# U weights' low parts by accumulating DMA during the gate build, and a scratch tensor for the first gate columns

## The chip, the cores and the metric

One core of a Trainium2 chip runs the kernel. The metric is the device time of one execution in microseconds (us). Before the change it is 1632.03 us, the median of three runs (1631.69 to 1634.06).

## The reference

One layer of a hybrid decoder trunk on 512 tokens of width 1024: state-space heads and attention heads side by side, an output projection and a normalisation, then a PEER mixer, and a last normalisation. The change lies in the mixer:

```python
q = (xb @ w_query).reshape(T, PEER_HEADS, 2, PEER_HALF_DIM)
s = jnp.einsum('thkd,hknd->thkn', q, sub_keys)
sv, si = lax.top_k(s, K)                       # K = 16, per half
...
top_s, top_pos = lax.top_k(cand_s, K)          # 16 of 256 candidate sums
expert_idx = jnp.take_along_axis(cand_i, top_pos, axis=-1)
gate = jax.nn.softmax(top_s, axis=-1)
u = jnp.take(u_table, expert_idx, axis=0)      # 16384 x 1024
act = jax.nn.gelu(jnp.einsum('td,thkd->thk', xb, u), approximate=False)
v = jnp.take(v_table, expert_idx, axis=0)
return jnp.einsum('thk,thkd->td', gate * act, v)
```

So each token has 128 experts (8 heads times 16), each with a gate.

## The kernel before

For the first 368 tokens (`NU`) the kernel doesn't gather experts. It computes the activations of all 16384 experts densely, in 128 *U chunks* of 128 experts, and multiplies them by a gate matrix that is zero except at the chosen experts; 128 *V chunks* then multiply the result by the V table. The last 16 tokens of the third block of 128 (`UG`) have their U part gathered row by row (`ug_index`, `ug_fetch`, `ug_dots`, `ug_head`), and the fourth block is gathered altogether during the V stage (`gather`).

**High and low parts.** Matmuls run on rounded 32-bit values (`F32R`). To keep accuracy, a weight tile `wir` of 128x1024 floats (512 KB) is split in two: ScalarE rounds it (`wih`, or `wihx` for each fourth tile), and another engine subtracts to get the remainder (`wil`). `mm3` then issues three matmuls, high times high, low activations times high weights, high activations times low weights; the low part is needed only in the third. The `Stream` class does the loads (on SP's DMA queue, three raw buffers), the roundings and the subtractions. When a chunk is about to be used, `get` has `splits` make the low part of the chunk two further on (`la = 2`, three `wil` buffers), and the rounding runs one more ahead (`ha = 1`). The subtraction is on GpSimd in the scoring stage and on VectorE from the index stage on (`lo_on`).

**A hand-written order.** The kernel is scheduled by hand: each engine runs its instructions in the order in which the program issues them. Two planner clocks, `tm[0]` for TensorE and `tm[1]` for VectorE, decide where U chunks go: `drive` issues a U chunk (`step_u`, 4.07 on TensorE's clock and, when VectorE subtracts, 1.2 on its own) whenever TensorE's clock isn't ahead, and otherwise the next piece of VectorE work. 54 U chunks (`LEAD`) come before the V stage, which then alternates U and V chunks.

**The stages around the change**, in order:

- *Index stage*, `stage2`: VectorE turns the chosen positions into expert indices, block by block (2, 0, 1, 3). After block 2 `ug_index` sends the indices of the 16 tokens to DRAM and back on GpSimd's queue (`ugi`, `ugg`, `uix`, `ugw`) and starts three row gathers (`urow`). After block 1 `g_head(0)` transposes indices and gates on TensorE and writes `ijT` and `gT`.
- *Gate build*, `build_g`: 48 steps of eight tokens. `hot` makes one-hot matrices on VectorE (`ij`, `g`; two buffers, one step ahead), 16 small matmuls form the gate columns, ScalarE copies them to `stg`, and after each fourth step SP stores 2 MB to the DRAM scratch `gsp`. The first 16 steps also each take the dot product of a gathered row (`urow`), and each frees its buffer for a further gather on GpSimd's queue.
- *Remaining U chunks* up to 54, then the V stage. `v_prep` multiplies activations by gate columns, which `load_g` reads back from `gsp` for four chunks at a time (`gt`), with the first two loads issued at the start of the V stage.

Of the kernel before, what the change touches and what calls it, by code (L numbers as in the profile page):

```python
# [11 lines left out]
F32 = mybir.dt.float32  # L12
# [5 lines left out]
AF = mybir.ActivationFunctionType  # L18
OP = mybir.AluOpType
AX = mybir.AxisListType  # L20
PSUM = bass.MemoryType.PSUM
# [9 lines left out]
NT = 384  # L31
UG = 16
NU = NT - UG
LEAD = 54
# [19 lines left out]
def tile_block(ctx: ExitStack, tc: tile.TileContext, I, out):  # L54
    nc = tc.nc
    ctx.enter_context(tc.manual_schedule())
    V, A, T, G = nc.vector, nc.scalar, nc.tensor, nc.gpsimd
# [3 lines left out]
    def pool(name, bufs=1, **kw):  # L61
        p = tc.alloc_tile_pool(name=name, bufs=bufs, **kw)
        opened.append(p)
        return p

    def close(*ps):
        for p in ps:
            opened.remove(p)
            p.release()

    def mm3(ps, lh, ll, rh, rl, start, stop):
        T.matmul(ps, lh, rh, start=start, stop=False)  # L72
        T.matmul(ps, lh, rl, start=False, stop=False)  # L73
        T.matmul(ps, ll, rh, start=False, stop=stop)  # L74

    def chain(*gs):
        for g in gs:
            yield from g

    class Stream:  # L80
        def __init__(self, p, name, srcs, shape, raw=2, la=1, lo=None, bufs=None):
            self.bufs = bufs or la + 1
            self.held, self.hold, self.place = (), None, {}
            self.lo = lo or (lambda n: V)
            self.p, self.name, self.srcs, self.shape, self.rawb, self.la = p, name, srcs, shape, raw, la
            self.raw, self.hi, self.w, self.nl, self.nh, self.ns, self.ha = {}, {}, {}, 0, 0, 0, 0
# [26 lines left out]
        def splits(self, m):  # L113
            while self.ns < min(m, len(self.srcs)):
                n = self.ns
                self.his(n + 1 + self.ha)
                r, h = self.raw.pop(n), self.hi.pop(n)
                l = self.tiles(n, 1)[:, :r.shape[-1]]
                self.lo(n).tensor_tensor(l, r, h, op=OP.subtract)  # L119
                self.w[n] = (h, l)  # L120
                self.ns += 1
                self.loads(n + 1 + self.rawb)
# [68 lines left out]

    dram = pool("dram", space=DRAM)
    xsp = dram.tile([NB, 128, D], F32, name="xsp")
    gsp = dram.tile([NT // 32, 128, 128, 32], F32, name="gsp")
    acd = dram.tile([64, 128], F32, name="acd")
    ugi = dram.tile([UG, 128], I32, name="ugi")
    ugg = dram.tile([UG, 128], F32, name="ugg")
# [26 lines left out]
    lo_on = [V]  # L224
# [14 lines left out]
    win = Stream(wst, "wi", items, [128, 1024], raw=3, la=2, lo=lambda n: lo_on[0])  # L239
    cnt = [0]  # L240

    def item():
        cnt[0] += 1
        return win.get(cnt[0] - 1)
# [17 lines left out]
    for p in range(2):  # L262
# [11 lines left out]
        for j, cs, act in (((0, slice(0, D), 1), (1, slice(0, D), 1)) if p == 0 else  # L274
                           ((0, slice(0, D), 0), (1, slice(0, 512), 1), (1, slice(512, D), 0))):
            t = XH[:, 2 * p + j, cs]
# [353 lines left out]
    for i in range(13, 18):  # L630
# [3 lines left out]
        q = qraw[i - 13] = wk.tile([128, S], F32, name="qr", bufs=5)  # L634
# [10 lines left out]
    for n in range(8):  # L645
# [3 lines left out]
        h, l = item()  # L649
# [89 lines left out]
    def qk_nope(h):  # L739
        wh, wl = item()  # L740
        ps = pp()
        for k in range(3):
            ks = slice(k * 128, k * 128 + 128)
            mm3(ps, wh[:, ks], wl[:, ks], qlh[:, k], qll[:, k], k == 0, k == 2)
        QN[h] = pair("qn")
        evac(ps, *QN[h])
        yield
        ps = pp()
        for k in range(2):
            ks = slice(384 + k * 128, 512 + k * 128)  # L750
            mm3(ps, wh[:, ks], wl[:, ks], kvh[:, k], kvl[:, k], k == 0, k == 1)
        KN[h] = pair("kn")
        evac(ps, *KN[h])
        yield
# [70 lines left out]
    g = chain(qk_nope(1), v_proj(0))  # L825
# [3 lines left out]
    for st in range(38):  # L829
        h, q = divmod(st, 4)  # L830
        if q == 0 and h:
            g = iter(())
            if h < 7:
                g = chain(qk_nope(h + 1), v_proj(h // 2)) if h % 2 == 0 else chain(q_pe(h // 2 + 1), qk_nope(h + 1))
# [34 lines left out]
    psX = pool("psX", bufs=2, space=PSUM)  # L869
    psW = pool("psW", bufs=4, space=PSUM)  # L870
# [227 lines left out]
    def build_g():  # L1098
        bc = [128, 4, 128, 2]

        def hot(n):
            ijT, gT = GT[n // 16]
            t0 = n % 16 * 8
            col = lambda z: z[:, t0:t0 + 8].rearrange("p (q c) -> p q c", c=2)[:, :, None, :].to_broadcast(bc)
            ij = gb.tile([128, 2, 4, 128, 2], F16, name="ij", bufs=2)
            g1 = gb.tile(bc, F16, name="g1", bufs=2)
            b2 = [128, 8, 128, 2]
            V.tensor_tensor(ij.rearrange("p e q i c -> p (e q) i c"), iotaE[:, None].to_broadcast(b2),  # L1108
                            ijT[:, n % 16].rearrange("p e (q c) -> p (e q) c", c=2)[:, :, None, :].to_broadcast(b2),
                            op=OP.is_equal)  # L1110
            oi, oj = ij[:, 0], ij[:, 1]
            V.tensor_tensor(g1, oi, col(gT[:, 1]), op=OP.mult)  # L1112
            V.tensor_tensor(oi, oi, col(gT[:, 0]), op=OP.mult)
            return oj, oi, g1

        nxt = hot(0)
        dots, head = ug_dots(), ug_head()
        tm[1] += 3.0
        yield 2.6
        for n in range(48):  # L1120
            b, g = divmod(n, 16)
            oj, oi, g1 = nxt
            if n < 47:
                nxt = hot(n + 1)
            if g % 4 == 0:
                stg = gb.tile([128, 128, 32], F32, name="stg", bufs=2)
            for hf in range(2):
                ps = pw()
                for t in range(4):
                    q, c = hf * 2 + t // 2, t % 2  # L1130
                    T.matmul(ps[:, t * 128:(t + 1) * 128], oj[:, q, :, c], oi[:, q, :, c], start=True, stop=False)
                    T.matmul(ps[:, t * 128:(t + 1) * 128], oj[:, q, :, c], g1[:, q, :, c], start=False, stop=True)
                q0 = g % 4 * 8 + hf * 4
                A.activation(stg[:, :, q0:q0 + 4],
                             ps.rearrange("p (t i) -> p i t", t=4), AF.Copy, scale=1.0 / GSC)
            tm[0] += 1.1
            if g % 4 == 3:
                for i in ((slice(0, 128),) if n < 47 else (slice(0, 8), slice(8, 128))):
                    nc.sync.dma_start(gsp[b * 4 + g // 4, :, i], stg[:, i])
            if g == 12 and b < 2:  # L1140
                g_head(b + 1)
            if n >= 1:
                tm[1] += next(dots, 0.0)
            if n in (30, 32, 34, 36, 38):
                tm[1] += next(head)
            yield 2.55 if n < 47 else 0.1
# [48 lines left out]
    def u_chunk(c, psum=None):  # L1195
        h, l = item()
        h = h.rearrange("p (k j) -> p k j", k=8)
        l = l.rearrange("p (k j) -> p k j", k=8)
        ps = (psum or pu)()[:, :NU]
        for k in range(8):  # L1200
            mm3(ps, h[:, k], l[:, k], XTH[:, k, :NU], XTL[:, k, :NU], k == 0, k == 7)
        ACT[c] = act_tile()
        A.activation(ACT[c][:, NU:], one, AF.Copy)
        A.activation(ACT[c][:, :NU], ps, AF.Gelu)  # L1204
# [5 lines left out]
    uc = 2  # L1210
# [26 lines left out]
    def step_u():  # L1237
        un[0] += 1
        u_chunk(un[0] - 1)
        tm[0] += T_U  # L1240
        if lo_on[0] is V:
            tm[1] += 1.2

    un = [uc]

    def drive(fill):
        while True:
            if tm[0] <= tm[1] and un[0] < (LEAD - RES if len(aps) > 1 else KEEP):
                step_u()
                continue  # L1250
            c = next(fill, None)
            if c is None:
                return
            tm[1] += c
# [24 lines left out]
    UR["g"] = ijp.tile([UG, 128], F32, name="ugw")  # L1279
    rt2 = pool("rt2")  # L1280
    lo_on[0] = V
    drive(stage2())
    close(rt2)
    close(rt)
    gb = pool("gb", side="right")
    UR["hd"] = gb.tile([128, UG], F32, name="uhd")
    UR["w"] = gb.tile([UG, 128], F32, name="uw")
    UR["m"] = gb.tile([UG, 2], F32, name="um")
    drive(build_g())
    uc = un[0]  # L1290
    while uc < LEAD:
        u_chunk(uc)
        uc += 1
    close(gb)
    close(psW)
    close(psX)

    psV = pool("psV", space=PSUM)
    va = [[psV.tile([128, 512], F32, name=f"va{b}{e}") for e in range(2)] for b in range(3)]
    vst = pool("vst")  # L1300
    gt = {}

    def load_g(q):
        if q < 32 and q not in gt:
            gt[q] = vst.tile([128, NT // 32, 4, 32], F32, name="gt", bufs=2)
            nc.sync.dma_start(gt[q], gsp[:, :, q * 4:(q + 1) * 4, :].rearrange("b j i t -> j b i t"))

    PP = {}

    pend = []  # L1310
# [23 lines left out]
    def v_lo():  # L1334
        if pend:
            c, P, Ph = pend.pop()
            Pl = v_sb(c, "Pl")
            V.tensor_tensor(Pl, P, Ph, op=OP.subtract)
            PP[c] = (Ph, Pl)

    def v_mm(b, c, hl, es=(0, 1)):
        Ph, Pl = PP[c]
        h, l = hl
# [250 lines left out]
```

## Time and profile before

| what | value |
|---|---|
| median of three runs | 1632.03 us |
| the profiled execution | 1631.69 us, span 1629.9 us |
| TensorE (PE) busy | 1582.4 us, 97% |
| VectorE (DVE) busy | 1376.6 us, 84% |
| ScalarE (ACT) busy | 699.2 us, 43% |
| GpSimd (POOL) busy | 467.8 us, 29% |
| DMA | 393.77 MB, mean 242 GB/s |

Busy time is what the profiler records for an engine; matmuls are pipelined, so that their recorded times overlap. "L119" is line 119 of the kernel. A row such as `wil<-wir,wih` names the output and the inputs by the program's tile names, followed by the shape and, in grouped views, the count, the total and the mean. In a timeline the first number is the start in us and the second the duration; a bracket at the end tells how long the engine stood idle before it and what ended the wait. POOL and SP rows named DMA are the issue of a transfer, not the transfer.

### The profile page before, as it was taken

To read this page: it belongs to the slowest core of one execution; us is meant where nothing else is said; L and a number is where in the kernel's file an instruction comes from. 1 tells how busy PE (TensorE), PEld (TensorE's weight loads), DVE (VectorE), ACT (ScalarE), POOL (GpSimd) and SP (SyncE) were. 2 spreads that over 40 slices of the span, in tenths; PEclk is the share of its full clock that TensorE was granted. 3 is DMA by queue.
4 is the path that set the end of the run, shared out by engine and by line. 5 is a ranking of instruction groups with operands and counts; after the bars stand their busy time and mean duration, and the time that the engine had idled before them with its cause. 6 is when DMAs were issued, how large, how long until landed. Compare 5 with 4: busy or idle time off the path is not lost.

```text
span 1629.9 us, 23745 instructions
## 1 busy us (share of the span) xinstructions
PE 1582.4 (97%) x8640; PEld 1394.0 (86%) x8640; DVE 1376.6 (84%) x2649; ACT 699.2 (43%) x1213; POOL 467.8 (29%) x332
## 2 busy tenths in 40 slices
PE   7999989999999999999899999999999999999997
PEld 5777868888888999998799999999999999888886
DVE  8979688947799999999588888888888888988977
ACT  5575466641433445555333333333333333333331
POOL 0000000000133113200155545555454544544300
PEclk9999999999999999999999999999999999999999
DMA  6242121364423368766799999999999999999973
GB/s 244 91 156 91 46 64 49 107 236 142 135 91 91 117 185 304 274 234 244 241 358 348 350 327 343 344 351 331 328 353 346 344 326 353 357 339 338 337 223 122
DMA packets 149020, 393.77 MB, mean 242 GB/s; under 512 B 12360, under 2 KB 63000, under 8 KB 147112
## 3 DMA queue, kind: packets, MB, share of 16 engines
q1 hardware_dynamic: 105816, 237.76, 43.1%
q0 software_dynamic: 42944, 154.24, 26.2%
q8 instruction: 67, 1.10, 0.3%
q14 instruction: 49, 0.40, 0.1%
q10 hardware_dynamic: 144, 0.26, 0.0%
HBM read 359.66 MB, written 31.51 MB: 240 GB/s over the span
## 4 chain that ended last, share of the span: by engine, by line
PE 72%; DVE 21%; ACT 2%; DMA 2%; issue 2%; SPq 0%; DVEq 0%; ACTq 0%
PE va L1347 10%; PE va L1351 10%; PE va L1348 10%; PE pu L72 8%; PE pu L74 8%; PE pu L73 8%; PE pa L72 3%; PE pa L74 3%; PE pa L73 3%; DVE wil L119 3%; DVE ij L1108 2%; DVE g L1112 1%; DVE t L952 1%; DVE urow L1053 1%; DVE ti L956 1%
## 5 line engine op out<-in xcount | busy, mean ns | idle before, releaser
L109 ACT ACTIVATE wih<-wir 128x1024 fp32r<-128x1024 f32 (+2 forms) x269 | 277.8, 1034 | 261.1 <-DMA wir<-v 87.4
L119 DVE TENSOR_TENSOR wil<-wir,wih 128x1024 fp32r<-128x1024 f32 (+1 forms) x254 | 302.1, 1190 | 103.4 <-ACT wih L109 47.2
L74 PE MATMUL pu<-XTH,wil 128*128 128x368 f32 x1008 | 331.7, 329 | 0.7 <-DVE wil L119 0.7
L72 PE MATMUL pu<-XTH,wih 128*128 128x368 f32 x904 | 298.8, 331 | 0.0
L73 PE MATMUL pu<-XTL,wih 128*128 128x368 f32 x904 | 296.8, 328 | 0.0
L1348 PE MATMUL va<-wil,Ph 128*128 128x512 f32 x726 | 283.5, 390 | 0.0
L1384 POOL DMA_INDIRECT row<-u,ix x128 | 189.9, 1484 | 231.2 <-DVE row L1395 135.7
L1384 POOL DMA_INDIRECT row<-v,ix x128 | 183.6, 1434 | 194.7 <-DVE ac L1401 165.5
L74 PEld LDWEIGHTS pu<-XTH,wil 128*128 128x128 f32 x1008 | 189.0, 188 | 1.3 <-DVE wil L119 1.3
L72 PEld LDWEIGHTS pu<-XTH,wih 128*128 128x128 f32 x904 | 169.7, 188 | 2.9
L73 PEld LDWEIGHTS pu<-XTL,wih 128*128 128x128 f32 x904 | 169.6, 188 | 2.9
L1347 PE MATMUL va<-wih,Ph 128*128 128x512 f32 x432 | 168.5, 390 | 0.0
L1401 DVE SCALAR_TENSOR_TENSOR ac<-row,hd,ac 128x1024 f32<-128x1024 f32 x128 | 164.1, 1282 | 2.5 <-DMA row<-v,ix 0.3
L1348 PEld LDWEIGHTS va<-wil,Ph 128*128 128x128 f32 x726 | 136.9, 189 | 26.1
L1204 ACT ACTIVATE act<-pu 128x368 f32<-128x368 f32 x126 | 60.0, 476 | 227.5 <-PE pu L74 193.3
L1395 DVE SCALAR_TENSOR_TENSOR row<-row,x 128x1024 f32<-128x1024 f32 x128 | 150.0, 1220 | 1.4 <-DMA row<-u,ix 1.4
L109 ACT ACTIVATE wihx<-wir 128x1024 fp32r<-128x1024 f32 x67 | 71.1, 1061 | 157.4 <-DMA wir<-v 124.6
L1351 PE MATMUL va<-wih,Pl 128*128 128x512 f32 x432 | 133.3, 390 | 0.0
L1347 PE MATMUL va<-wihx,Ph 128*128 128x512 f32 x294 | 115.9, 394 | 4.8 <-ACT Ph L1331 4.8
L119 DVE TENSOR_TENSOR wil<-wir,wihx 128x1024 fp32r<-128x1024 f32 x62 | 75.9, 1224 | 52.3 <-issue 47.8
L1351 PEld LDWEIGHTS va<-wih,Pl 128*128 128x128 f32 x432 | 81.1, 188 | 17.3
L1347 PEld LDWEIGHTS va<-wih,Ph 128*128 128x128 f32 x432 | 81.1, 188 | 15.7
(458 smaller groups left out, 3072.6 us busy)
## 6 DMA issues: line engine op xcount, KB each, us to landing
wir<-ut SPq DMA_DIRECT2D x128, 512.0 KB
wir<-v SPq DMA_DIRECT2D x128, 512.0 KB
gt<-gsp SPq DMA_DIRECT2D x32, 768.0 KB
gsp<-stg SPq DMA_DIRECT2D x11, 2048.0 KB
wir<-wo SPq DMA_DIRECT2D x26, 512.0 KB
wir<-wf SPq DMA_DIRECT2D x18, 512.0 KB
wir<-wqr SPq DMA_DIRECT2D x16, 512.0 KB
de<-acd POOLq DMA_DIRECT2D x8, 512.0 KB
```

What stands on the lines that cost most here:

```text
L72: T.matmul(ps, lh, rh, start=start, stop=False)
L73: T.matmul(ps, lh, rl, start=False, stop=False)
L74: T.matmul(ps, ll, rh, start=False, stop=stop)
L109: A.activation(h, r, AF.Copy)
L119: self.lo(n).tensor_tensor(l, r, h, op=OP.subtract)
L1204: A.activation(ACT[c][:, :NU], ps, AF.Gelu)
L1347: T.matmul(va[b][e], Ph[:, bs], h[:, cs], start=c == 0, stop=False)
L1348: T.matmul(va[b][e], Ph[:, bs], l[:, cs], start=False, stop=False)
L1351: T.matmul(va[b][e], Pl[:, bs], h[:, cs], start=False, stop=c == 127)
L1384: G.indirect_dma_start(out=R[s], out_offset=None, in_=I["u"] if s < 128 else I["v"], in_offset=bass.IndirectOffsetOnAxis(ap=ix[:, s % 128: ...
L1395: V.scalar_tensor_tensor(r, r, 1.0, x3, op0=OP.mult, op1=OP.mult, accum_out=hd[:, s:s + 1])
L1401: V.scalar_tensor_tensor(ac, r, hd[:, s - 128:s - 127], ac, op0=OP.mult, op1=OP.add)
```

## The change

While a new flag `add` of the stream is set, the low part is made in another way: ScalarE writes the negated high part into `wil`, and a DMA on GpSimd's queue reads the weight tile from DRAM a second time and adds it there. The flag is set for the index stage and the gate build and cleared before the remaining U chunks. While it is set, the planner charges VectorE nothing for a U chunk.

The first eight gate columns go to a DRAM tensor of their own, `gs0`, so each group of gate columns is stored by two DMAs. The two `stg` buffers move into pools of their own, and the pool of the V stage is opened and the first two `gt` loads (which read `gs0`) are issued right after the gate build, ahead of the remaining U chunks.

```diff
+                if self.add:
+                    A.activation(l, h, AF.Copy, scale=-1.0)
+                    G.dma_start(l, self.srcs[n], accum_op=OP.add)
+                else:
+                    self.lo(n).tensor_tensor(l, r, h, op=OP.subtract)
-                self.lo(n).tensor_tensor(l, r, h, op=OP.subtract)
...
+    gs0 = dram.tile([NT // 32, 128, 8, 32], F32, name="gs0")
+    gsp = dram.tile([NT // 32, 128, 120, 32], F32, name="gsp")
-    gsp = dram.tile([NT // 32, 128, 128, 32], F32, name="gsp")
...
+                stg = gs[n // 4 % 2].tile([128, 128, 32], F32, name="stg")
-                stg = gb.tile([128, 128, 32], F32, name="stg", bufs=2)
...
+                nc.sync.dma_start(gs0[b * 4 + g // 4], stg[:, 0:8])
+                nc.sync.dma_start(gsp[b * 4 + g // 4], stg[:, 8:])
-                for i in ((slice(0, 128),) if n < 47 else (slice(0, 8), slice(8, 128))):
-                    nc.sync.dma_start(gsp[b * 4 + g // 4, :, i], stg[:, i])
...
+        if lo_on[0] is V and not win.add:
-        if lo_on[0] is V:
             tm[1] += 1.2
...
     lo_on[0] = V
+    win.add = True
     drive(stage2())
     close(rt2)
     close(rt)
+    gs = [pool(f"gs{i}", side="right") for i in (1, 0)][::-1]
     gb = pool("gb", side="right")
...
     drive(build_g())
+    close(gb, *gs)
+    vst = pool("vst")
+    gt = {}
...
+            src, q0 = (gs0, q * 4) if q < 2 else (gsp, q * 4 - 8)
+            nc.sync.dma_start(gt[q], src[:, :, q0:q0 + 4, :].rearrange("b j i t -> j b i t"))
+
+    for q in range(2):
+        load_g(q)
+    win.add = False
     uc = un[0]
     while uc < LEAD:
         u_chunk(uc)
         uc += 1
-    close(gb)
```

More of the change, by code (lines that the diff above doesn't have):

```diff
@@ L82, in __init__ @@
             self.bufs = bufs or la + 1
-            self.held, self.hold, self.place = (), None, {}
+            self.held, self.hold, self.place, self.add = (), None, {}, False
             self.lo = lo or (lambda n: V)
@@ L1289, in tile_block @@
     drive(build_g())
[L1290 to L1293, printed above, removed]
-    close(gb)
[L1295 to L1299, printed above, removed]
+    close(gb, *gs)
     vst = pool("vst")
@@ L1305, in load_g @@
             gt[q] = vst.tile([128, NT // 32, 4, 32], F32, name="gt", bufs=2)
-            nc.sync.dma_start(gt[q], gsp[:, :, q * 4:(q + 1) * 4, :].rearrange("b j i t -> j b i t"))
+            src, q0 = (gs0, q * 4) if q < 2 else (gsp, q * 4 - 8)
[3 more added lines that the diff above has]
+    win.add = False
+    uc = un[0]
+    while uc < LEAD:
+        u_chunk(uc)
+        uc += 1
+    close(psW)
+    close(psX)
+    psV = pool("psV", space=PSUM)
+    va = [[psV.tile([128, 512], F32, name=f"va{b}{e}") for e in range(2)] for b in range(3)]
     PP = {}
```

## The prediction

> **What bounds the kernel now.** I read the span first, then a table of stages, then what TensorE waited for.
>
> ```profile
> span 1629.9 us, 23745 instructions
> 546.00:598.00 52.00, 51.32 (x307) 50.69 (x306) 51.42 (x78) 24.73 (x49) 7.10 (x7) 1.00 0.51 155
> 598.00:660.00 62.00, 62.00 (x494) 60.23 (x493) 61.05 (x76) 33.57 (x65) 16.79 (x10) 1.00 0.75 264
> 660.00:720.00 60.00, 56.96 (x502) 54.50 (x501) 58.91 (x72) 33.34 (x65) 6.26 (x5) 1.00 0.74 268
> 720.00:786.00 66.00, 59.99 (x559) 56.90 (x558) 61.28 (x76) 36.47 (x72) 0.48 (x1) 1.00 0.66 234
> 786.00:806.00 20.00, 15.18 (x77) 14.00 (x76) 5.27 (x8) 6.31 (x13) 0.00 (x0) 0.83 0.73 237
> 806.00:1560.00 754.00, 754.00 (x3783) 672.93 (x3782) 634.93 (x802) 279.88 (x446) 374.62 (x258) 1.00 0.96 340
> ```
>
> Columns after the stretch: its length, PE, PEld, DVE, ACT and POOL busy, clock, DMA share, GB/s. From 806 us TensorE never stops, so whatever moves the beginning of that V stage moves the end one for one. From 546 us to there lie the index stage (stage2) and the gate build, where VectorE is as full as TensorE and TensorE, from 660 us, is not full.
>
> ```profile
> PE pw L1131 <- DVE ij L1113: 7.9, 9, 1.5
> PE va L1347 <- ACT Ph L1331: 4.8, 1, 4.8
> PE pw L1131 <- ACT stg L1134: 1.1, 5, 0.2
> PE pu L74 <- DVE wil L119: 0.7, 2, 0.4
> 801.95 0.80 PE L1347 MATMUL va<-wihx,Ph 128*128 128x512 f32 x1 [4.82 <-ACT Ph L1331]
> 807.17 0.39 PE L1347 MATMUL va<-wihx,Ph 128*128 128x512 f32 x1
> 807.40 0.40 PE L1348 MATMUL va<-wil,Ph 128*128 128x512 f32 x1
> 808.10 0.33 PE L72 MATMUL pu<-XTH,wih 128*128 128x368 f32 x1
> ```
>
> These are TensorE's waits (total, times, longest) and its timeline at the stage border. The waits add up to 14.5 us. After the 4.8 us gap TensorE restarts at a lower clock (0.83 in the fifth stretch): 18 V matmuls take 808.10 - 801.95 = 6.15 us where the recovered pitch of 0.23 gives 4.1. So some 16.5 us is all there is to win, and at full pitch the V stage begins at 808.10 - 4.1 = 804.0. That is the moment I recompute.
>
> **The change part by part.** 33 low parts (wil) leave VectorE; each becomes a negating copy on ScalarE and a 512 KB accumulating DMA from GpSimd's queue.
>
> ```profile
> L119 DVE TENSOR_TENSOR wil<-wir,wih 128x1024 fp32r<-128x1024 f32 x25 | 30.5, 1219 | 0.0
> L119 DVE TENSOR_TENSOR wil<-wir,wihx 128x1024 fp32r<-128x1024 f32 x8 | 9.8, 1220 | 0.0
> 540.50 0.48 ACT L1204 ACTIVATE act<-pu 128x368 f32<-128x368 f32 x1 [2.47 <-PE pu L74]
> 544.50 0.48 ACT L1204 ACTIVATE act<-pu 128x368 f32<-128x368 f32 x1 [2.47 <-PE pu L74]
> 544.88 1.05 ACT L109 ACTIVATE wih<-wir 128x1024 fp32r<-128x1024 f32 x1
> 550.11 1.23 DVE L119 TENSOR_TENSOR wil<-wir,wih 128x1024 fp32r<-128x1024 f32 x1
> 568.48 1.22 DVE L119 TENSOR_TENSOR wil<-wir,wih 128x1024 fp32r<-128x1024 f32 x1
> 569.61 0.29 DVE L1036 SCALAR_TENSOR_TENSOR p<-ijg 128x128 int32<-128x128 f32 x1
> ```
>
> The first two rows group VectorE's work from 600.6 to 783.8: 25 + 8 = 33 subtractions lie in the gate build before. One holds VectorE for 569.61 - 568.48 = 1.14 us, so 37.6 us leave it there. A Gelu waits for each U chunk, so a chunk is 544.50 - 540.50 = 4.0 us of TensorE. The copies, priced like the rounding copy at 1.05, add 35 us to a ScalarE that is about half idle; they lie beside TensorE.
>
> The planner no longer charges VectorE for a U chunk and places fewer of them between gate steps: 12 instead of 14 before the first gate transposes, 3 instead of 5 after, and 15 instead of 3 behind the last gate matmul (one of them inside the V loop).
>
> *The queue.* GpSimd works in order. Four accumulates (chunks 7 to 10 of the run of 12) come first, then the index exchange and three row gathers, and only then chunk 11's accumulate.
>
> ```profile
> 570.19 0.53 POOL L1037 DMA_DIRECT2D ugi<-p  x1 [27.08 <-DVE p L1036]
> 573.78 0.63 POOL L1039 DMA_DIRECT2D uix<-ugi  x1 [2.56 <-DMA ugi<-p]
> 577.95 1.37 POOL L1047 DMA_INDIRECT urow<-u,uix  x1 [3.05 <-DMA uix<-ugi]
> 581.63 1.87 POOL L1047 DMA_INDIRECT urow<-u,uix  x1 [0.30 <-issue]
> 420.52 2.65 DMA xsp<-xm
> 560.18 5.04 DMA wir<-ut
> 585.53 0.49 PE L1089 MATMUL px<-ident,ijg 128*128 128x128 f32 x3
> 589.86 0.29 DVE L1095 SCALAR_TENSOR_TENSOR gT<-px,gT 128x128 f16<-128x128 f32 x1
> 600.66 1.22 DVE L1108 TENSOR_TENSOR ij<-iotaE,ijT 128x2048 f16<-128x2048 f16 x1
> 783.97 0.23 PE L1131 MATMUL pw<-ij 128*128 128x128 f16 x1 [1.49 <-DVE ij L1113]
> 784.87 0.41 PE L72 MATMUL pu<-XTH,wih 128*128 128x368 f32 x1
> ```
>
> In brackets is how long an engine stood and for what: GpSimd itself stands for the index to land. The exchange holds it from 570.19 to 583.50, 13.3 us; today nothing is queued behind. Without the five subtractions from 550.11 to 568.48 VectorE makes the index 5.7 us earlier, at 563.9 to 564.2, so GpSimd is free again at 577.5. No accumulate is in the trace. The nearest 512 KB rows land in 2.65 (a store, alone) and 5.04 us (the U load of the same stage); reading its destination too it might take twice the latter, 10.1. I take 5.0, the load among the same traffic: chunk 11's low part lands at 582.5 and TensorE starts the chunk at 582.2, since its first two matmuls need only the high part. Unhindered it would start at 528.5 + 40 = 568.5 (chunk 4 ended at 544.50). So TensorE loses some 14 us here, whatever it loses earlier in that run.
>
> Chunks 11 and 12 end at 590.2; the transposes follow (585.53 before), then a Gelu and two small copies on ScalarE, about 1.8 us, so VectorE gets gT at 592.0. From gT to the first one-hot are 600.66 - 589.86 = 10.8 us today, three subtractions among them; 7.4 remain. The gate build starts at 599.4, 1.3 earlier than today, though VectorE alone would allow 600.66 - 13 x 1.14 = 585.8.
>
> From the first one-hot to the last gate step it takes 783.97 - 600.66 = 183.3, less 37.6, so 145.7: at 745.1. TensorE has 22 chunks and 48 steps of 0.9 (783.97 to 784.87) there, 131 us, plus three chunks, from 591: it is done sooner and VectorE still sets the pace. Then 0.9 + 15 x 4.0 = 60.9: the V stage begins at 806.0, 2.0 later than 804.0.
>
> *The traffic.* 33 accumulates read 17.3 MB again.
>
> ```profile
> 642.50:645.00 2.50, 2.50 (x23) 2.50 (x21) 2.43 (x4) 2.28 (x5) 0.59 (x1) 1.00 1.00 429
> L1053 DVE SCALAR_TENSOR_TENSOR urow<-urow,ux 128x1024 f32<-128x1024 f32 x16 | 19.5, 1218 | 0.0
> ```
>
> At a full share this stretch moved 429 GB/s. A gate step alone takes VectorE (145.7 - 16 x 1.14) / 48 = 2.7 us, the first 16 with a gathered row (last line) 3.8. Each of these brings 0.52 MB of row, 0.52 of gate store, and 9 chunks in 16 steps bring 0.29 of load and 0.29 of accumulate, or 0.59 if the destination's reading counts: 1.62 to 1.92 MB, at that rate 3.8 to 4.5 us. Over 16 steps that is 0 to 11 us of stretch; the 32 later steps, without a row, add up to 4 by the same count. I take 4, nearer the low end, because TensorE has spare time there and stores may trail into the last 60 us. In the V stage nothing is accumulated, so its 96% DMA share stays. Sum: +2.0 + 4 = +6.
>
> [...] No run so far shows an accumulate.
>
> *The scratch tensor.* The first gate loads wait for the small stores only and are issued ahead of 14 U chunks, 56 us, so the 4.8 us gap and its 2.0 of slow clock vanish; that is already in the 60.9, and would cost 6.9 if the cover failed. Gate stores go from 12 to 24 on SP's queue, beside other work: 0.
>
> Against the profiled execution (1631.69 us; span 1629.9; the median of the three runs shown, 1632.03, is 0.3 more) this gives 1631.7 + 6 = 1638 us.
>
> **The rivals.**
>
> *A, faster:* the accumulates keep ahead of TensorE and the index exchange does not hold them. Then the gate build starts at 585.8 and the V stage at 585.8 + 145.7 + 60.9 = 792.4, 11.6 earlier: 1620. For it: VectorE bounds these stages, and the gap at the border goes in any case. Against it: GpSimd's 2.56 and 3.05 us of standing on its own DMAs. It decides if chunk 11's low part lands before about 570.
>
> *B, the DMA becomes the bound:* an accumulate lands in 10.1 us and counts double. Chunk 11 starts 5.1 later and the gate build stretches by 15: 2.0 + 5.1 + 15 = +22, 1654. For it: 1.00 of share at 429 GB/s already today. Against: the mean there is 264 to 268.
>
> *C, no change to be seen:* an accumulate lands in 2.65 us and stores trail freely; 2.0 - 2.4 + 0 = 0, 1632. Saved and lost time cancel.
>
> **How the numbers follow.** About 0.2% (3.3 us) is what a measurement of this kernel can tell from no change. Forecast (1635.3 to 1648) 0.41, B 0.20, C 0.17, A 0.22; so slower 0.61, same 0.17, faster 0.22. The costs not seen span 0 (C) to +22 (B) for the queue's own mechanism, 1632 to 1654; to leave out no more than two in ten, the range goes to 1622 on A's side and 1660 on B's.
>
> **What would show it.** Right: GpSimd goes from the index exchange straight to accumulates near 578; TensorE waits some 10 us or more for wil there; the first one-hot comes near 599, the last gate step near 745 to 750; no gap at the V stage, which begins near 810 and runs as before. Wrong: a first one-hot near 586 (A), or TensorE and VectorE both waiting on DMA through the gate build (B).

## The result, and the profile after

The changed kernel takes 1683.89 us, the median of four runs (1680.05 to 1684.67), against 1632.9 us before it on the same chips (1631.69 to 1634.06). The ratio is 1.0309, with a 95% interval of 1.0296 to 1.0322: it is slower, by 51 us. The direction was forecast; the size, +6 us, was not, and the time lies outside the range.

The windows of the profile after, of the stretch from 546 us to the V stage (columns as before: length, busy time of PE, PEld, DVE, ACT and POOL, clock, DMA share, GB/s), with the span from its page:

```profile
span 1682.6 us, 23803 instructions
546.00:600.00 54.00, 34.31 (x180) 33.40 (x178) 34.24 (x71) 23.97 (x40) 12.95 (x14) 0.81 0.79 194
600.00:620.00 20.00, 17.78 (x126) 16.99 (x126) 14.07 (x15) 11.90 (x23) 3.37 (x4) 1.00 0.92 205
620.00:660.00 40.00, 32.51 (x264) 31.01 (x263) 31.55 (x43) 22.90 (x39) 17.32 (x13) 0.91 0.90 292
660.00:706.00 46.00, 34.83 (x275) 32.57 (x273) 31.02 (x43) 23.42 (x44) 14.19 (x12) 0.89 1.02 318
706.00:760.00 54.00, 45.09 (x441) 43.11 (x442) 47.43 (x62) 35.17 (x64) 6.80 (x10) 1.00 0.92 282
760.00:800.00 40.00, 34.38 (x326) 32.70 (x325) 28.72 (x35) 25.47 (x46) 3.67 (x5) 1.00 1.03 317
800.00:856.00 56.00, 54.39 (x327) 54.09 (x326) 17.15 (x18) 20.79 (x43) 0.00 (x0) 1.00 0.54 171
856.00:1612.00 756.00, 756.00 (x3793) 674.66 (x3792) 635.55 (x803) 282.17 (x450) 376.41 (x258) 1.00 0.96 339
```

VectorE did become free, as meant: it is busy 34.24 of the first 54 us, where it was full before. But TensorE is busy only 34.31 there too. Neither engine sets the pace any longer; what is full is the DMA, at shares of 0.79 to 1.03 up to 800 us where it was 0.51 to 0.75 (a share over 1.00 shows that it is no strict measure). From 856 us on the V stage runs as it did, so all of the loss lies ahead of it. What TensorE waited for, five places of its timeline, and VectorE's one-hots of the first and the 17th gate step:

```profile
PE pu L74 <- DMA wil<-ut: 40.0, 13, 12.9
PE pw L1136 <- DVE ij L1118: 15.1, 9, 1.9
PE pu L72 <- ACT act L1209: 1.6, 1, 1.6
559.61 0.67 PE L74 MATMUL pu<-XTH,wil 128*128 128x368 f32 x1 [5.28 <-DMA wil<-ut]
592.22 0.68 PE L74 MATMUL pu<-XTH,wil 128*128 128x368 f32 x1 [12.88 <-DMA wil<-ut]
602.34 0.49 PE L1094 MATMUL px<-ident,ijg 128*128 128x128 f32 x3
611.32 1.22 DVE L1113 TENSOR_TENSOR ij<-iotaE,ijT 128x2048 f16<-128x2048 f16 x1
685.10 1.22 DVE L1113 TENSOR_TENSOR ij<-iotaE,ijT 128x2048 f16<-128x2048 f16 x1
792.93 0.23 PE L1136 MATMUL pw<-ij 128*128 128x128 f16 x1
856.40 0.39 PE L1358 MATMUL va<-wihx,Ph 128*128 128x512 f32 x1
```

Of 310.4 us from 546.0 to the first V matmul at 856.4, some 241.5 are work (804.0 - 546.0 before, less the 16.5 lost there). Of the 68.9 lost, 40.0 + 15.1 + 1.6 are these waits, the first of them for accumulates. The rest, about 12, is the clock behind the stalls: an estimate from the table, PE's busy time times what the clock lacks, gives 34.31 x 0.19 + 32.51 x 0.09 + 34.83 x 0.11 = 13.3. Two short windows, one from the end of the 12.88 us stall and one after it, show that:

```profile
592.20:596.00 3.80, 3.78 (x12) 3.78 (x13) 0.00 (x0) 0.00 (x0) 0.00 (x0) 0.50 0.99 195
596.00:600.00 4.00, 4.00 (x22) 4.00 (x21) 0.00 (x0) 1.47 (x3) 0.00 (x0) 0.83 0.05 9
```

The granted clock was 0.50 for the first 3.8 us after the stall and 0.83 in the next four. Now GpSimd's queue around that stall (the number after the bracket's opening is how long GpSimd stood), and below it four of the eight accumulates that lie on the profile's chain of waits (issue, time to landing):

```profile
549.01 0.93 POOL L121 DMA_DIRECT2D wil<-ut  x1 [4.36 <-ACT act L1208]
567.89 0.85 POOL L121 DMA_DIRECT2D wil<-ut  x1 [7.50 <-ACT act L1208]
568.43 0.86 POOL L1042 DMA_DIRECT2D ugi<-p  x1
575.51 0.64 POOL L1044 DMA_DIRECT2D uix<-ugi  x1 [5.71 <-DMA ugi<-p]
579.75 1.03 POOL L1052 DMA_INDIRECT urow<-u,uix  x1 [3.10 <-DMA uix<-ugi]
584.65 2.79 POOL L121 DMA_DIRECT2D wil<-ut  x3
```

```profile
549.01 10.56 DMA wil<-ut
584.65 7.53 DMA wil<-ut
682.85 16.52 DMA wil<-ut
738.10 9.69 DMA wil<-ut
```

The index exchange does stand between two accumulates: three pile up behind it and are issued together at 584.65. And the eight accumulates on the chain land 7.3 to 16.5 us after their issue. The chain holds the landings that something waited for; what the other 25 of the 33 took isn't shown.

### The profile page after: what moved, and what is told of

The parts are those of the page before. It is cut to its first block, busy times and chain, and to the rows that moved or that the text cites. A ratio compares the mean times of both kernels' runs of the same rounds, so it can differ in the third digit from the quotient of the medians.

```text
span 1682.6 us, 23803 instructions
## 1 busy us (share of the span) xinstructions
PE 1592.6 (95%) x8640; PEld 1403.2 (83%) x8640; DVE 1343.0 (80%) x2616; ACT 729.8 (43%) x1246; POOL 497.3 (30%) x365
## 4 chain that ended last, share of the span: by engine, by line
PE 84%; DMA 6%; DVE 5%; issue 2%; ACT 2%; POOL 1%; DVEq 0%; POOLq 0%; ACTq 0%
PE va L1358 10%; PE va L1362 10%; PE va L1359 10%; PE pu L74 10%; PE pu L72 10%; PE pu L73 10%; DMA wil<-ut 5%; PE pw L73 3%; PE pw L74 3%; PE pa L72 3%; PE pw L72 3%; PE pa L73 3%; PE pa L74 3%; PE pb L496 1%; PE px L945 1%
## 5 line engine op out<-in xcount | busy, mean ns | idle before, releaser
L74 PE MATMUL pu<-XTH,wil 128*128 128x368 f32 x1008 | 337.3, 335 | 40.0 <-DMA wil<-ut 40.0
L123 DVE TENSOR_TENSOR wil<-wir,wih 128x1024 fp32r<-128x1024 f32 (+1 forms) x229 | 271.5, 1187 | 129.1 <-ACT wih L109 53.0
L74 PEld LDWEIGHTS pu<-XTH,wil 128*128 128x128 f32 x1008 | 192.4, 191 | 43.9 <-DMA wil<-ut 43.9
L123 DVE TENSOR_TENSOR wil<-wir,wihx 128x1024 fp32r<-128x1024 f32 x54 | 66.1, 1224 | 61.1 <-issue 44.2
L1358 PEld LDWEIGHTS va<-wih,Ph 128*128 128x128 f32 x432 | 81.2, 188 | 15.7
```

The costliest lines, as they stand in the source:

```text
L1358: T.matmul(va[b][e], Ph[:, bs], h[:, cs], start=c == 0, stop=False)
```

## The experiments

Three theories stood at the start. The *adding* is the cost: an accumulating DMA asks twice the engine time. The *queue and the traffic* are: accumulates stand behind other work on GpSimd's in-order queue, or land late among the other transfers, against a look-ahead of two chunks. Or the *planner*, which no longer charges VectorE, has put the chunks in bad places. Where no interval is given, a time is one execution; the kernel before, run beside them, read 1631.4 to 1634.4, and the four executions of the changed kernel lie 4.6 us apart, so that a difference of under 5 us between single executions says little.

**The scratch tensor alone.** The accumulates are switched off; the scratch tensor, the pools and the early gate loads stay.

```diff
-    win.add = True
+    win.add = False
```

> Keeps the scratch tensor, its pools and the early gate loads, and takes the accumulating DMAs out (VectorE subtracts, and the planner charges it, as before). Theory 1 (an accumulate lands too late for a look-ahead of two chunks) and theory 2 (GpSimd's queue makes it late): all of the loss belongs to the accumulates, and what is left gives back the gap at the V stage, 4.8 us of standing and 2.0 of slow clock: 1625 to 1629. Rival: the doubled stores or the other layout of the scratch cost time themselves: over 1633.

Measured: 1628.8 us, the median of seven runs, against 1633.6; ratio 0.9971 (0.9959 to 0.9982). From its waits of TensorE:

```profile
PE pw L1136 <- DVE ij L1118: 7.8, 8, 1.5
PE va L1358 <- ACT Ph L1342: 1.7, 1, 1.7
```

The gap at the V stage went from 4.8 to 1.7 us, and the clock no longer falls behind it (1.00 in the windows from 760 to 856 us). This half of the change is a gain, and it makes the version that beats both kernels. The other half costs the 51 us and the 4.8 won here besides.

**The planner's charge put back.**

```diff
-        if lo_on[0] is V and not win.add:
+        if lo_on[0] is V:
```

> Accumulates as in the changed kernel, but the planner charges VectorE 1.2 per U chunk as before, so the U chunks stand between the gate steps as before the change and the last 15 no longer stand alone. Theory 3 (the loss is the planner's: 61 us of U chunks behind the gate build with VectorE idle): most of it comes back, 1640 to 1655. Theories 1 and 2: about 13 more chunks need an accumulate, each late by about 1.2 us (40 us of waits over 33), and the tail is shorter: 1680 to 1700, with more than 40 us of TensorE waiting for wil.

Measured: 1688.49 us. With as many chunks between the gate steps as before, 45 chunks have an accumulate instead of 33, and the waits grow instead of shrinking:

```profile
PE pu L74 <- DMA wil<-ut: 48.8, 19, 12.2
```

So the planner's charge is not the cause: more chunks in the gate build only mean more accumulates that TensorE waits for.

**An accumulate by itself.** A small kernel on 512 KB tiles: copies and accumulates one at a time, then eight of each at once.

> No part of the reference is computed: only DMAs of 512 KB tiles by themselves, each landing shown by a one-column copy on VectorE: one after the other from SP, from GpSimd, from GpSimd with add, the same at half the width; then eight at once without and with add, and eight adds beside eight loads from SP. Theory 1 with a fixed latency: an add alone lands in 8 us or more against 3 to 4 for a copy, eight at once take little longer than eight copies (about 11 us). Theory 1 with a rate (the destination is read too): an add alone takes about 2 us more than a copy, and eight at once take twice the time of eight copies, some 22 us. Theory 2: add and copy alike.

Measured, on the chain of waits one copy and one accumulate alone, both from GpSimd:

```profile
34.50 3.44 DMA one<-u
42.61 5.10 DMA one<-u
```

And VectorE's timeline reading the tiles as they land, three of the eight copies and three of the eight accumulates:

```profile
84.61 0.15 DVE L32 COPY r<-t 128x1 f32<-128x1 f32 x1 [1.32 <-DMA t<-u]
85.88 0.15 DVE L32 COPY r<-t 128x1 f32<-128x1 f32 x1 [1.11 <-DMA t<-u]
87.15 0.15 DVE L32 COPY r<-t 128x1 f32<-128x1 f32 x1 [1.12 <-DMA t<-u]
...
98.23 0.15 DVE L32 COPY r<-t 128x1 f32<-128x1 f32 x1 [2.31 <-DMA t<-u]
100.70 0.15 DVE L32 COPY r<-t 128x1 f32<-128x1 f32 x1 [2.32 <-DMA t<-u]
103.26 0.15 DVE L32 COPY r<-t 128x1 f32<-128x1 f32 x1 [2.40 <-DMA t<-u]
```

Alone, an accumulate lands in 5.1 us (5.02 to 5.25 in four), the value that the prediction took for it in the kernel. Of the four copies from GpSimd the last two took 3.44 and 3.58 us; the first two, 7.37 and 4.49, came right behind the issue of the eight loads from SP (17.87 to 21.86 us), which so didn't run beside the last accumulates as meant. An accumulate of half the width lands in 3.6 us. In a row accumulates land 2.5 us apart where copies land 1.27 apart: half the rate, the first theory in its form with a rate. Beside four stores on SP's queue the last accumulates came 3.8 us apart, about the sum of the two.

**A plain copy in the accumulate's place.** It overwrites the negated copy, so the low part is the weight itself.

```diff
-                    G.dma_start(l, self.srcs[n], accum_op=OP.add)
+                    G.dma_start(l, self.srcs[n])
```

> The same DMA on the same queue at the same place with the same bytes read from DRAM, but it overwrites instead of adding, so the low part is the weight itself and the products are not the reference's. Theory 1: a plain copy lands in about 5 us, TensorE's waits for wil fall from 40 to about 12 (the index exchange alone), 1638 to 1648. [...]

Measured: 1672.49 us, with 25.1 us of waits for wil. So the adding is 11 us of the 51; 40 us stay with a transfer that adds nothing, as the second theory had it, by which the time was to be over 1670. The four copies on this run's chain of waits landed in 7.0 to 10.7 us, so a transfer lands late here without adding too.

**The index exchange on SP's queue.** Its four DMAs no longer stand ahead of chunk 11's accumulate; the row gathers still do.

```diff
-        G.dma_start(ugi, ix[128 - UG:])
+        nc.sync.dma_start(ugi, ix[128 - UG:])
...
-        G.dma_start(UR["g"], ugg)
+        nc.sync.dma_start(UR["g"], ugg)
```

> The four index-exchange DMAs that stood ahead of the accumulate of chunk 11 on GpSimd's queue (12.88 us of TensorE's standing) are issued on SP's queue instead. If the order on GpSimd's queue is the cause of that stall, the stall of 12.88 us before the first matmul of chunk 11 goes to under 4 us, waits on DMA wil<-ut fall from 40.0 us to 27-30, and with the slow clock behind the stall the time falls by 12 to 18 us, to 1666-1672. If the landing under load is the cause whatever stands ahead on the queue, the stall stays over 8 us and the time is 1678-1688.

Measured: 1675.28 us, 8.6 less. The stall shrank but stayed, now behind the gathers alone:

```profile
584.79 0.67 PE L74 MATMUL pu<-XTH,wil 128*128 128x368 f32 x1 [8.42 <-DMA wil<-ut]
```

That lies between the two expectations: the place in the queue counts, and is a minor part.

**A look-ahead of three**, with a buffer more. The room for it comes from three U chunks fewer ahead of the V stage, and so it has a control of its own. The rounding stays three chunks ahead, as it was.

```diff
-LEAD = 54
-KEEP = 43
+LEAD = 51
+KEEP = 40
...
-            if k == 0 and self.ha and n % 4 == 3:
-                return self.xp.tile(self.shape, F32R, name=self.name + "hx", bufs=1)
+            if self.ha and n % 4 == 3:
+                return self.xp.tile(self.shape, F32R, name=self.name + "hl"[k] + "x", bufs=1)
...
+    win.la = 3
```

> Control of e7_la3: the changed kernel with three U chunks fewer ahead of the V stage (LEAD 51 and KEEP 40, which makes the room that a third buffer needs). Three chunks move behind, no wait of the gate build changes by either theory: DMA wil<-ut at 35-45 us, time within 8 us of the changed kernel's 1684 (1676-1692).

> The low parts are begun three chunks ahead, with one buffer more. If the landing is a matter of delay only (each accumulate lands 7 to 16 us after its issue but the DMA engines have room), the waits on DMA wil<-ut fall from 40 us to under 15 (the one behind the index exchange and little else) and the time is 25 to 40 us under the control's. If the DMA engines are full in this stretch (share 0.8 to 1.0), starting earlier only moves the queueing: waits over 30 us and a time within 8 us of the control's.

Measured: the control 1679.55 us, three ahead 1671.98, so 7.6 less; 25 to 40 were expected if delay was all, under 8 if the engines were full. Its waits of TensorE:

```profile
PE pw L1136 <- DVE ij L1118: 26.8, 15, 3.7
PE pu L74 <- DMA wil<-ut: 18.5, 4, 13.3
```

The waits for accumulates halve, and most of what is left is the index exchange's one stall. But TensorE now waits 26.8 us for one-hots, and VectorE stands 17.6 us for gathered rows that land late (6.4 in the control). The lateness went in part to other transfers. **Both together**:

> Look-ahead of three and the index exchange on SP's queue together. If the two are separate costs they add up: 1672.0 less 8.6 is 1663, within 3, with waits on DMA wil<-ut of 4-8 us, all that is left of the waits TensorE had on the accumulates; what stays over the kernel before (some 30 us) then lies in VectorE's one-hots (15-27 us of TensorE's waits). If the wait only moves from the exchange to the chunk behind it, wil stays over 14 us and the time at 1668-1673.

Measured: 1663.40 us, the sum that was forecast; but the waits for wil were 19.7 us and not 4 to 8, one stall of 11.46 among them. Four accumulates stood on GpSimd's queue behind the first three row gathers. The time hit and its stated reason did not.

**Accumulates in the gate build alone** (the flag is set after the index stage):

> Accumulating DMAs in the gate build alone; in the stage before it the low parts stay on VectorE as in the kernel before. If the lateness that the earlier stage gathers (first one-hot 611.3 against 600.7) is carried to the end, the first one-hot comes at 598-602 and the time is 1670-1675. If the gate build is bound by its own accumulates whatever it starts with, it runs as long as in the changed kernel from its earlier begin (181.6 us), which is the same sum; it stays at 1680-1686 if the gain in the earlier stage is given back by chunks that are moved into the gate build.

Measured: 1668.32 us, 15.6 less, a little more than expected. The first one-hot comes at 602.2 us instead of 611.3, but that is not what is gained: the last gate step begins at 793.38, no earlier than the 792.93 of the changed kernel. The gain lies behind it, where 46.96 us pass before the V stage (793.38 to 840.34) and not 63.47: four chunks fewer are left, by an estimate at 4.0 us each, because more stood ahead. The time is 39.5 us over that of the scratch tensor alone, so the larger part of the loss belongs to the gate build.

**Half the bytes**: the accumulate adds the left half of each tile; the right half of a low part stays the negated rounded weight.

```diff
-                    G.dma_start(l, self.srcs[n], accum_op=OP.add)
+                    G.dma_start(l[:, :512], self.srcs[n][:, :512], accum_op=OP.add)
```

> The accumulate adds the left half of each tile alone; the right half of a low part stays the negated rounded weight. Half the bytes in the adding DMAs, with the same number of issues, waits and queue places. If bytes in the DMA engines set the cost, waits on DMA wil<-ut fall under 15 us and the time comes to 1645-1660, below the plain copy of full width (1672.5). If places in the queue and the look-ahead set it, waits stay over 25 us and the time is 1668-1680.

Measured: 1667.35 us, with 25.6 us of waits: the time lies between the two ranges, the waits are those of the second theory. By the rates of the small kernel it asks about the same engine time as the plain copy (an estimate: half of 2.5 us against 1.27), and it comes within about 5 us of it.

**Accumulates that nobody reads.** Low parts on VectorE; copies and accumulates of the same kind go to two spare tiles. The planner charges VectorE again, so 39 chunks have one and not 33.

```diff
+                    d = self.xp.tile(self.shape, F32R, name=self.name + "dx", bufs=2)[:, :r.shape[-1]]
+                    A.activation(d, h, AF.Copy, scale=-1.0)
+                    G.dma_start(d, self.srcs[n], accum_op=OP.add)
```

> Control of e10_spare: low parts on VectorE everywhere, no accumulates, six chunks fewer ahead of the V stage (LEAD 48, KEEP 37, room for two spare tiles). Both theories: 1624-1640, no waits of TensorE over 8 us beyond the one-hots'.

> Low parts on VectorE as in the control; beside them the same negated copies and accumulating DMAs for the same chunks as in the changed kernel go to two spare tiles that TensorE never reads. The work is left over: nothing computed uses it. If the cost of the change is TensorE waiting for the sums themselves (latency against the look-ahead), the time is within 8 us of the control's. If the traffic and the queues are the cost (what SP's loads and GpSimd's gathers lose beside the accumulates), the time is 20 us or more over the control's, with VectorE and ScalarE waiting for wir and urow.

Measured: the control 1644.46 us, above its 1640 (six chunks fewer ahead of the V stage cost more than thought), the run 1680.40: 36 more though TensorE reads none of the sums. It doesn't settle the matter, since two spare tiles were too few:

```profile
ACT widx L121 <- DMA widx<-ut: 32.5, 15, 13.2
PE pu L72 <- ACT act L1209: 19.4, 6, 9.8
```

ScalarE stood 32.5 us until a spare tile had landed, and TensorE then waited for ScalarE. The same late landing was waited for at another place. ScalarE also waited 55.6 us for raw loads, 28.3 in the control, as the second theory expected; how much of the 36 that makes isn't shown.

**GpSimd's queue for accumulates alone.** The sixteen row gathers are left out (three loads of fixed rows on SP's queue stand in for them, reused by the later dot products), and the index exchange is on SP's queue. A control without accumulates, then the run, then the run with three ahead, then with plain copies:

> Control of the next three: low parts on VectorE, no accumulates; the row gathers of the last sixteen tokens are left out (three loads of fixed rows in place of sixteen gathers by index) and the index exchange is on SP's queue, so GpSimd's queue carries nothing else in this stretch. Every theory: within 8 us of the kernel without accumulates (1628.8).

> The changed kernel with the same gathers left out and the index exchange on SP's queue: GpSimd's queue carries accumulates alone. If the places in GpSimd's queue are the main cause (accumulates behind gathers that wait for VectorE), the waits on DMA wil<-ut fall from 40 us under 12 and the time comes within 15 us of its control's (1630-1645). If the DMA engines' time is the main cause, waits stay over 20 us and the time is 25 us or more over its control's (1655-1675).

> The same with the look-ahead of three. If what is left is the delay of each landing against the look-ahead, waits on DMA wil<-ut are under 4 us and the time is within 8 us of the control's. If the DMA engines are full, it gives less than 5 us against the run with two ahead.

> The same with look-ahead two and a plain copy in place of the sum (the low part becomes the weight itself): half the engine time. If the DMA engines' double time is what is left, it comes within 8 us of the control's and 10 us or more under the run with the sums. If places in the queue were all, it equals the run with the sums within 5 us.

Measured: control 1629.53 us, run 1656.21, three ahead 1641.51, copies 1645.19. The run is 26.7 us over its control, as expected if the engines' time is the main cause; its waits for wil, 16.8 us, lie between the two expectations. The copies come 11.0 us under the sums and stay 15.7 over the control: the adding is a part of what is left, not all. Three ahead is 14.7 us under two ahead, which speaks for the delay of each landing. But it has LEAD 51, and so a control of that size was run too:

> Control of the run with look-ahead three and the queue alone, at the same LEAD 51 and KEEP 40, low parts on VectorE: every theory 1626-1638, so that the remainder of the look-ahead run (1641.5) is 4 to 15 us.

Measured: 1639.72 us, just above its range. The run with three ahead is 1.8 us over this control, which single executions don't tell from nothing, and 12.0 over the control with LEAD 54. The smaller number flatters the accumulates: three chunks fewer cost the kernel without accumulates 10.2 us, while the changed kernel lost nothing by them (1679.55 against 1683.89). The end of the gate build in the two controls, LEAD 54 first:

```profile
760.00:786.00 26.00, 22.51 (x224) 21.07 (x222) 24.07 (x30) 14.71 (x28) 0.00 (x0) 1.00 0.66 239
760.00:786.00 26.00, 18.45 (x175) 16.38 (x174) 23.66 (x29) 11.56 (x22) 0.00 (x0) 0.67 0.48 191
```

With LEAD 51 TensorE has less to do here, and its clock falls to 0.67 though no wait here is over 1.9 us, while VectorE stays as busy. The V stage begins only 1.8 us earlier (799.61 against 801.37), though some 12 us of chunks (an estimate, three at 4.0) have moved behind. Held against the two controls, the accumulates so cost 1.8 to 12.0 us with three ahead. Waits of TensorE with two ahead and then with three:

```profile
PE pu L74 <- DMA wil<-ut: 16.8, 8, 4.6
PE pw L1138 <- DVE ij L1120: 15.1, 9, 1.9
```

```profile
PE pw L1138 <- DVE ij L1120: 16.0, 10, 1.9
PE pu L74 <- DMA wil<-ut: 5.3, 2, 2.8
```

With nothing else on GpSimd's queue there is no stall over 4.6 us, and 27.7 of the 51 us come back. Without accumulates the gathers cost nothing (1628.8 us with them, 1629.53 without), so they cost only together with the accumulates. What the 27.7 were, order or bytes, was still open, since the gathers' 8 MB went too. **The bytes put back**, as loads of fixed rows on SP's queue into a spare tile:

```diff
-            UR[n] = ug.tile([128, D], F32, name="urow", bufs=3)
-            G.indirect_dma_start(out=UR[n], out_offset=None, in_=I["u"],
-                                 in_offset=bass.IndirectOffsetOnAxis(ap=UR["ix"][:, n:n + 1], axis=0))
+            r = ug.tile([128, D], F32, name="urow", bufs=2) if n < 2 else ug.tile([128, D], F32, name="uspare")
+            nc.sync.dma_start(r, I["u"][n * 128:(n + 1) * 128])
+            UR[n] = UR["k", n] = r if n < 2 else UR["k", n % 2]
```

> The run with GpSimd's queue for accumulates alone left out the gathers' 512 KB each as well. Here the same bytes are moved, as direct loads of fixed rows on SP's queue into a spare tile that nothing reads (two real tiles stay for the dot products). If the order on GpSimd's queue was the cause, the time stays within 5 us of that run's 1656.2 (1651-1661), the waits on DMA wil<-ut under 20 us. If the gathers' bytes were the cause, it goes back by 10 us or more, to 1666-1684, with waits over 27 us.

Measured: 1677.72 us, back up by 21.5, with time and waits as expected if the bytes were the cause. The stall at the index exchange did not return (3.27 us at 582.92 instead of 12.88 at 592.22), but waits did, on TensorE and, for the raw loads, on ScalarE:

```profile
PE pu L74 <- DMA wil<-ut: 28.1, 10, 6.1
ACT wih L109 <- DMA wir<-ut: 42.1, 7, 9.3
667.85 10.70 SPq L1052 DMA_DIRECT2D uspare<-u  x2
```

GpSimd's queue had nothing but accumulates here, so the order on that queue alone is not the main cause. The run has a flaw of its own: the spare loads go into one tile one after the other and stand ahead of raw loads on SP's queue (two issues took 10.70 us), so part of the 21.5 may be SP's order. These loads without accumulates, the bytes on a queue of their own, and the same bytes with three ahead and GpSimd's queue free weren't tried.

## Why the prediction was wrong

*What held.* TensorE and VectorE set the pace before, and the V stage moved with its beginning. The 33 subtractions left VectorE, whose busy time over the whole kernel fell by 33.6 us (1376.6 to 1343.0; 37.6 were counted). The index exchange and the gathers held chunk 11's accumulate and TensorE stood for it, 12.88 us where 14 were forecast; that the length fits is in part luck, since the stall began and ended some 10 us later than forecast (579.3 to 592.2 instead of 568.5 to 582.2). Behind the gate build lay 63.5 us (792.93 to 856.40) where 60.9 were forecast. The scratch tensor gave 4.8 us; 6.9 were taken.

*The step that failed* is "the traffic", with the term "I take 4", together with "I take 5.0" for a landing. From the first one-hot to the last gate step it took 792.93 - 611.32 = 181.6 us; the forecast was 145.7 + 4. The first one-hot itself came at 611.3 and not 599.4, 11.9 later. The terms stand so: 11.9 + (181.6 - 145.7) + (63.5 - 60.9) = 50.4, of which 4 were forecast; that is the miss of 46. Of the 35.9 by which the gate build outran its 145.7, 13.0 fall on the first 16 steps (685.10 - 611.32 = 73.8 us, where 16 steps of 3.8 are 60.8) and 22.9 on the later 32, where no row is gathered and the forecast allowed 4.

Why the landing was wrong: 5.0 is right for an accumulate alone (5.1), and on the chain of waits it takes 7.3 to 16.5. The notice is short besides: two chunks of 4.0 us look like 8, but the issue comes behind a Gelu, a rounding and the copy on ScalarE. The first accumulate was issued at 549.01 and its sum was wanted at 559.61 - 5.28 = 554.33, after 5.3 us, which a landing of 5.0 just meets and the 10.56 that it took does not. Why the traffic was wrong: bytes per gate step were set against the highest rate seen, 429 GB/s, while from 660 to 800 us the engines moved 282 to 318 GB/s at shares of 0.92 to 1.03; eight accumulates by themselves moved 211 GB/s at a share of 1.06 (small kernel, 93 to 116 us). Counted over the whole stretch, rows that lay on the table say more, as an estimate. By the DMA shares of before, the engines were busy 52 x 0.51 + 62 x 0.75 + 60 x 0.74 + 66 x 0.66 + 20 x 0.73 = 175.6 of 260 us; 84.4 were free. A 512 KB transfer at the 429 GB/s quoted takes 1.22 us, an accumulate by the prediction's upper count twice that, and 33 of them 80.6. So the change asked for 95% of all idle DMA time in a stretch where each transfer has a due time. After it, the same sum of shares to 856 us is 265.1, or 89.5 more than before: 2.7 us for each accumulate.

In the small kernel accumulates landed 2.5 us apart and copies 1.27, so the upper counts of the prediction (0.59 MB for a gate step's accumulates and not 0.29) were the ones to take.

The rival "the DMA becomes the bound" had the mechanism, with a landing of 10.1 and a double count, and was still short: +22 against the +52.7 of the profiled executions. It let the gate build stretch by 15 where it stretched by 36, and like the forecast it left out the clock behind the stalls (0.50 in the first 3.8 us behind that of 12.88 us), some 12 us.

*The forecast of the exchange's end*, 577.5, was 7.2 us early. VectorE made the index at 566.04 and not at 563.9, and the exchange was issued at 568.43 only, behind chunk 10's accumulate, before which GpSimd had stood 7.50 us for ScalarE; there the Gelus wait for TensorE, which came out of its first stall, 5.28 us, at 559.61. So a late landing delays the issue of the accumulates after it. Then the exchange and the gathers took 16.2 us and not 13.3 to let the next accumulate go, at 584.65.

*What the runs settle.* No single wait is the cause. The exchange's place is worth 8.6 us, the adding 11, one chunk more of notice 7.6 (14.7 where the gathers are gone, with LEAD 51 in it), the index stage 15.6, the gathers with their places 27.7, and these overlap. Shown is that the accumulates, with their copies, are the whole loss (1628.8 us without them), and that little of it is left, 1.8 to 12.0 us, once both the gathers are out and the notice is three chunks; either alone leaves 26.7 (the gathers out) or 32 to 42 us (three ahead: 1671.98 against 1639.72 and 1629.53). How the gathers' part divides between bytes and queues stays open.

## What to carry to other kernels

Before work is moved from an engine to the DMA, multiply (1 - share) by the length of the very stretch and compare it with the new transfers' engine time, an accumulate at twice a copy's (2.5 against 1.27 us in the small kernel). Here, at 95% of it, a lone landing of 5 us became 7.3 to 16.5 where something waited for it. Then hold that loaded landing, not the lone one, against the notice from the issue to the use (here 5.3 us and not 8), and list what stands ahead on the issuing queue. A change of two parts is worth trying in halves: here the small half alone was faster than either kernel.

## What the runs showed that had not been expected

In the small kernel accumulating DMAs went at half the rate of copies when eight ran together (2.5 against 1.27 us for 512 KB), but one alone took only some 1.4 to 1.5 times as long (5.10 against 3.44 and 3.58). DMA engines at a share near 1 need not hold TensorE up: with three ahead and the gathers out, the engines were this full from 546 to 760 us, and TensorE waited 5.3 us for accumulates, not 40.0:

```profile
546.00:600.00 54.00, 45.69 (x273) 44.55 (x272) 44.97 (x70) 35.35 (x59) 11.54 (x12) 0.97 0.98 247
620.00:660.00 40.00, 39.70 (x340) 38.18 (x339) 39.25 (x55) 30.57 (x52) 6.04 (x7) 1.00 1.04 323
706.00:760.00 54.00, 46.88 (x443) 45.17 (x441) 40.12 (x52) 35.59 (x64) 5.64 (x7) 1.00 1.00 309
```

TensorE is busy 39.70 of the middle 40 us, at full clock, with the DMA share at 1.04.
